# Combining two experts' outputs on one core: a new pitch of the partitions in HBM, an early activation table and last stores from SyncE

## The chip, the cores and the metric

The kernel runs on one core of a Trainium2 chip. The metric is the device time in microseconds (us) of one execution; less is better. Partitions are the 128 rows of the on-chip memory SBUF. HBM is the memory off the core, from which DMA engines bring data in and to which they take results. Each core has 16 DMA engines, and two queues feed them here: q1, filled by SyncE (SP), and q10, filled by ScalarE (ACT).

## The reference

Each of 16 x 1024 tokens has two vectors of 512 floats, the outputs of two experts, and two weights. The result is their weighted sum.

```
batch, seq, hidden, k = 16, 1024, 512, 2
weights = combine_weights[..., np.newaxis]                    # (16, 1024, 2, 1)
return np.sum(expert_outputs * weights, axis=2)               # (16, 1024, 512) float32
```

So 67.1 MB come in, 33.6 MB go out, and every loaded value is used once.

## The kernel before

The 16384 tokens are laid over the 128 partitions in blocks: partition p holds tokens 128 p to 128 p + 127. A token is 4 KB of input and 2 KB of output, so in HBM neighbouring partitions lie 512 KB apart in the input and 256 KB apart in the output; this distance is the pitch. The loop runs over 16 tiles, and each takes the next J = 8 tokens of every partition: 32 KB per partition in (`et`, 4 MB), 16 KB per partition out (`ot`, 2 MB).

The weights come as one table `wt` of 128 x 256 floats, with one DMA issued from ACT (L43). Loads of `et` are issued from SP (L48), stores from ACT (L66). `et` and `ot` have four buffers each. A load thus waits until DVE has read the buffer's last user, four tiles earlier; a tile's computation waits for its load, and for the store of four tiles before to have left the `ot` buffer. Instructions stand on each engine in the order in which the program writes them, so an engine that waits holds up all that it has to do later, its DMA issues included.

For a token, a first instruction writes the first vector times its weight to `ot`: on VectorE (DVE) as a scaling (L57), and in the last tile (g = 15) on ACT as an ACTIVATE with a scale (L55). A second one on DVE (L58) adds the other vector times its weight. ACT needs an activation table before its first ACTIVATE, and the compiler puts that load (ACT_TABLE_LOAD) right ahead of it. A tile is stored whole, but the last one in parts of 4, 2 and 2 tokens.

In what follows "store 14" is the store of tile 14, the last that is stored whole. Lines L43 to L66 are those of the kernel before; in the changed kernel L54 loads the table, L61 loads `et`, L70 is the ACTIVATE, L72 and L73 are DVE's two steps, and L82 stores.

Of the kernel before, what the change touches and what calls it, by code (L numbers as in the profile page):

```python
# [1 line left out]

# [4 lines left out]


@with_exitstack
def kernel(  # L10
    ctx: ExitStack,
    tc: tile.TileContext,
    expert_outputs: bass.AP,
    combine_weights: bass.AP,
    out: bass.AP,
):


    nc = tc.nc
    b, s, k, h = expert_outputs.shape  # L20
    assert k == 2
    n = b * s
    P = nc.NUM_PARTITIONS
    per = n // P
    assert per * P == n
    eo = expert_outputs.rearrange("b s k h -> (b s) (k h)").rearrange("(p t) f -> p t f", p=P)
    cw = combine_weights.rearrange("b s k -> (b s) k").rearrange("(p t) k -> p (t k)", p=P)
    o = out.rearrange("b s h -> (b s) h").rearrange("(p t) f -> p t f", p=P)

    dt = mybir.dt.float32  # L30
    mult = mybir.AluOpType.mult
    add = mybir.AluOpType.add

    J = 8
    copy = mybir.ActivationFunctionType.Copy
    last = per // J - 1

    wpool = ctx.enter_context(tc.tile_pool(name="w", bufs=1))
    ipool = ctx.enter_context(tc.tile_pool(name="in", bufs=4))
    opool = ctx.enter_context(tc.tile_pool(name="out", bufs=4))  # L40

    wt = wpool.tile([P, per * k], dt)
    nc.scalar.dma_start(out=wt, in_=cw)  # L43

    for g in range(per // J):
        et = ipool.tile([P, J, k * h], dt)
        ot = opool.tile([P, J, h], dt)
        nc.sync.dma_start(out=et, in_=eo[:, g * J : (g + 1) * J, :])  # L48
        c0 = 0
        for c in (4, 2, 2) if g == last else (J,):  # L50
            for i in range(c0, c0 + c):
                t = g * J + i
                w0, w1 = wt[:, 2 * t : 2 * t + 1], wt[:, 2 * t + 1 : 2 * t + 2]
                if g == last:  # L54
                    nc.scalar.activation(out=ot[:, i, :], in_=et[:, i, 0:h], func=copy, scale=w0)  # L55
                else:
                    nc.vector.tensor_scalar_mul(out=ot[:, i, :], in0=et[:, i, 0:h], scalar1=w0)  # L57
                nc.vector.scalar_tensor_tensor(  # L58
                    out=ot[:, i, :],
                    in0=et[:, i, h : 2 * h],  # L60
                    scalar=w1,  # L61
                    in1=ot[:, i, :],
                    op0=mult,
                    op1=add,
                )
            nc.scalar.dma_start(  # L66
                out=o[:, g * J + c0 : g * J + c0 + c, :], in_=ot[:, c0 : c0 + c, :]
            )
            c0 += c


# [1 line left out]
_INS = ['expert_outputs', 'combine_weights']  # L73
_OUTS = [((16, 1024, 512), 'float32')]


# [23 lines left out]
```

## Time and profile before

| what | value |
|---|---|
| median of 3 runs | 241.34 us (241.24 to 241.75) |
| the profiled execution, its own time | 241.88 us |
| its span | 240.1 us |
| DVE busy | 133.8 us (56%) |
| ACT busy | 6.4 us (3%) |
| mean over the span | 420 GB/s |
| an `et` load, issue to landing, median | 49.6 us (4096 KB) |
| a whole `ot` store, issue to landing, median | 24.9 us (2048 KB) |

The span runs from the first to the last instruction in the trace; the time of an execution holds a little more. The DMA share is the mean busy share of the 16 DMA engines. Packets are the pieces into which a DMA is cut for one engine: here one partition's row, 32 KB of a load or 16 KB of a store.

### The profile page before, as it was taken

What the parts mean: (1) busy time and instruction counts of PE and PEld (TensorE: products, weight loads), DVE (VectorE), ACT (ScalarE), POOL (GpSimd) and SP (SyncE); (2) the same over time, 40 slices, a digit from 0 to 9 for tenths busy, and PEclk for the clock granted to TensorE, in tenths of its full rate; (3) what the DMA queues carried; (4) which work ended last, traced back from release to release, by engine and by line L of the source; (5) the groups of instructions that cost most, each with busy time, mean ns of one, the idle gap of its engine ahead of it and who ended that gap; (6) DMA issues with size and microseconds to landing.
All of it is one profiled execution on the core that took longest, in us unless ns stands there. A gap on an engine that the chain in (4) does not pass through costs nothing.

```text
span 240.1 us, 377 instructions
## 1 busy us (share of the span) xinstructions
DVE 133.8 (56%) x248; ACT 6.4 (3%) x9; POOL 0.2 (0%) x4
## 2 busy tenths in 40 slices
DVE  0068937729185490945819276391853919549062
ACT  0000000000000000000000000000000000000072
POOL 0000000000000000000000000000000000000000
DMA  7999999999999999999999999999999999999967
GB/s 267 439 434 431 355 434 456 414 431 437 437 423 445 439 409 426 456 415 453 420 437 431 415 448 423 431 450 437 435 423 434 420 429 442 418 450 437 412 296 304
DMA packets 5042, 100.81 MB, mean 420 GB/s; under 512 B 560, under 2 KB 688, under 8 KB 944
## 3 DMA queue, kind: packets, MB, share of 16 engines
q1 hardware_dynamic: 2304, 67.11, 65.4%
q10 hardware_dynamic: 2736, 33.69, 32.9%
q14 instruction: 2, 0.02, 0.0%
HBM read 67.24 MB, written 33.55 MB: 420 GB/s over the span
## 4 chain that ended last, share of the span: by engine, by line
DMA 56%; DVE 26%; another core or an unknown queue 13%; issue 1%; ACT 1%; SPq 0%; ACTq 0%; DVEq 0%
DMA et<-in_expert_outputs_dram 56%; DVE ot L58 16%; DVE ot L57 10%; ACT ot L55 1%; ACT L55 1%; SPq L48 0%; ACTq L66 0%; DVEq L95 0%; DVEq L57 0%; ACTq L55 0%
## 5 line engine op out<-in xcount | busy, mean ns | idle before, releaser
L57 DVE TENSOR_SCALAR ot<-et,wt 128x512 f32<-128x512 f32 x120 | 52.7, 482 | 93.4 <-DMA et<-in_expert_outputs_dram 79.5
L58 DVE SCALAR_TENSOR_TENSOR ot<-et,wt,ot 128x512 f32<-128x512 f32 x128 | 90.0, 746 | 9.3 <-ACT ot L55 9.3
L55 ACT ACT_TABLE_LOAD x1 | 1.3, 1283 | 227.8 <-DMA et<-in_expert_outputs_dram 227.8
L55 ACT ACTIVATE ot<-et,wt 128x512 f32<-128x512 f32 x8 | 5.1, 709 | 1.5 <-DVE ot L58 1.5
L84 POOL MEMSET const-bfloat16-1.0<- 128x1 bf16 x1 | 0.1, 101 | 0.0
L84 POOL MEMSET const-uint8-127<- 128x1 uint8 x1 | 0.1, 101 | 0.0
L84 POOL MEMSET const-float32-0.0<- 128x1 f32 x1 | 0.1, 98 | 0.2 <-issue 0.2
L84 POOL MEMSET const-float32-1.0<- 128x1 f32 x1 | 0.1, 98 | 0.0
## 6 DMA issues: line engine op xcount, KB each, us to landing
et<-in_expert_outputs_dram SPq DMA_DIRECT2D x16, 4096.0 KB, 49.6
out_dram<-ot ACTq DMA_DIRECT2D x15, 2048.0 KB, 24.9
out_dram<-ot ACTq DMA_DIRECT2D x1, 1024.0 KB, 3.9
out_dram<-ot ACTq DMA_DIRECT2D x2, 512.0 KB, 3.2
wt<-in_combine_weights_dram ACTq DMA_DIRECT2D x1, 128.0 KB, 13.2
```

Source lines behind the costliest of these rows:

```text
L55: nc.scalar.activation(out=ot[:, i, :], in_=et[:, i, 0:h], func=copy, scale=w0)
L57: nc.vector.tensor_scalar_mul(out=ot[:, i, :], in0=et[:, i, 0:h], scalar1=w0)
L58: nc.vector.scalar_tensor_tensor(out=ot[:, i, :], in0=et[:, i, h : 2 * h], scalar=w1, in1=ot[:, i, :], op0=mult, op1=add,)
L84: nc = _bacc.Bacc("TRN2", target_bir_lowering=False, num_devices=1)
```

## The change

The first 15360 tokens are laid over the partitions with 120 tokens each, so that the pitch is 480 KB in and 240 KB out; they make tiles 0 to 14. The last 1024 tokens are laid out on their own with 8 tokens per partition, at a pitch of 32 KB in and 16 KB out; they make tile 15. The table is loaded in two DMAs accordingly, 960 B and 64 B per partition, both from ACT. The first token of tile 0 is scaled by an ACTIVATE on ACT, with which the activation table's load moves to the start of the kernel. The last tile is stored in four parts of two tokens, issued from SP and not from ACT.

```diff
-    eo = expert_outputs.rearrange("b s k h -> (b s) (k h)").rearrange("(p t) f -> p t f", p=P)
-    cw = combine_weights.rearrange("b s k -> (b s) k").rearrange("(p t) k -> p (t k)", p=P)
-    o = out.rearrange("b s h -> (b s) h").rearrange("(p t) f -> p t f", p=P)
+    J = 8
+    main = per - J
+    eo = expert_outputs.rearrange("b s k h -> (b s) (k h)")
+    cw = combine_weights.rearrange("b s k -> (b s) k")
+    o = out.rearrange("b s h -> (b s) h")
+
+    def rows(x):
+        a = x[0 : P * main, :].rearrange("(p t) f -> p t f", p=P)
+        b = x[P * main : n, :].rearrange("(p t) f -> p t f", p=P)
+        return lambda t, c: a[:, t : t + c, :] if t < main else b[:, t - main : t - main + c, :]
+
+    eo, cw, o = rows(eo), rows(cw), rows(o)
...
-    nc.scalar.dma_start(out=wt, in_=cw)
+    for t, c in ((0, main), (main, J)):
+        nc.scalar.dma_start(
+            out=wt[:, k * t : k * (t + c)].rearrange("p (t k) -> p t k", k=k), in_=cw(t, c)
+        )
...
-        nc.sync.dma_start(out=et, in_=eo[:, g * J : (g + 1) * J, :])
+        nc.sync.dma_start(out=et, in_=eo(g * J, J))
         c0 = 0
-        for c in (4, 2, 2) if g == last else (J,):
+        for c in (2, 2, 2, 2) if g == last else (J,):
...
-                if g == last:
+                if t == 0 or g == last:
                     nc.scalar.activation(out=ot[:, i, :], in_=et[:, i, 0:h], func=copy, scale=w0)
...
-            nc.scalar.dma_start(
-                out=o[:, g * J + c0 : g * J + c0 + c, :], in_=ot[:, c0 : c0 + c, :]
+            (nc.sync if g == last else nc.scalar).dma_start(
+                out=o(g * J + c0, c), in_=ot[:, c0 : c0 + c, :]
             )
```

More of the change, by code (lines that the diff above doesn't have):

```diff
@@ L32 @@
     add = mybir.AluOpType.add
-    J = 8
     copy = mybir.ActivationFunctionType.Copy
```

## The prediction

> **What bounds the kernel now.** I read the page first: the busy line, the DMA rows, then the queues.
>
> ```profile
> DVE 133.8 (56%) x248; ACT 6.4 (3%) x9; POOL 0.2 (0%) x4
> DMA  7999999999999999999999999999999999999967
> q1 hardware_dynamic: 2304, 67.11, 65.4%
> q10 hardware_dynamic: 2736, 33.69, 32.9%
> HBM read 67.24 MB, written 33.55 MB: 420 GB/s over the span
> ```
>
> No compute engine is busy for more than 56%. The 16 DMA engines are: q1 (loads) and q10 (stores and the weight table) hold 65.4 + 32.9 = 98.3% of 16 x 240.1 us, so 236.0 us of the 240.1 us on a mean DMA engine. Only 4.1 us per engine are not transfer. The kernel is bound by DMA from end to end, and what the change can win lies in those 4.1 us or in packets that last longer than they must.
>
> For the second I go to the trace's single DMA records. Of the 2048 load packets of 32 KB at least three in four last exactly 1213 ns, the shortest; all stores of 16 KB lie between 611 and 626 ns. 32 KB in 1213 ns is 27.0 GB/s, times 16 it is 432 GB/s. So at the present 512 KB pitch nearly every packet already takes one fixed minimum. Sorted by engine (each engine's packets abut, so they can be strung together), the excess over 1213 ns is alike on all: about 0.69 us in the very first load packet, about 0.74 us in the load packets around the first store (23 to 28 us), then nearly nothing, 1.57 us on a mean engine in all. The second patch is the one dip of the GB/s row, in the second line below; the windows also show the hole at the end:
>
> ```profile
> 0.00:6.00 6.00, 0.00 (x0) 0.00 (x0) 0.20 (x4) 1.00 0.74 268
> 24.00:30.00 6.00, 6.00 (x12) 0.00 (x0) 0.00 (x0) 1.00 0.93 355
> 210.00:216.00 6.00, 2.82 (x6) 0.00 (x0) 0.00 (x0) 1.00 1.04 448
> 228.00:231.00 3.00, 1.15 (x2) 2.99 (x5) 0.00 (x0) 1.00 0.98 421
> 231.00:234.00 3.00, 2.92 (x5) 1.88 (x4) 0.00 (x0) 1.00 0.42 175
> 234.00:237.00 3.00, 1.42 (x2) 1.33 (x2) 0.00 (x0) 1.00 0.99 404
> ```
>
> The last two columns are the DMA share and GB/s. From 231 to 234 us the share is 0.42: 0.58 x 3 = 1.7 us of hole per mean engine. The timeline says why:
>
> ```profile
> 221.78 0.34 ACTq L66 DMA_DIRECT2D out_dram<-ot  x1
> 227.81 1.28 ACT L55 ACT_TABLE_LOAD   x1 [227.81 <-DMA et<-in_expert_outputs_dram]
> 229.10 3.78 ACT L55 ACTIVATE ot<-et,wt 128x512 f32<-128x512 f32 x6
> 229.85 4.07 DVE L58 SCALAR_TENSOR_TENSOR ot<-et,wt,ot 128x512 f32<-128x512 f32 x6 [8.11 <-ACT ot L55]
> 232.63 1.66 ACTq L66 DMA_DIRECT2D out_dram<-ot  x2
> 234.34 1.33 ACT L55 ACTIVATE ot<-et,wt 128x512 f32<-128x512 f32 x2 [1.46 <-DVE ot L58]
> 235.09 1.42 DVE L58 SCALAR_TENSOR_TENSOR ot<-et,wt,ot 128x512 f32<-128x512 f32 x2 [1.17 <-ACT ot L55]
> 236.54 0.34 ACTq L66 DMA_DIRECT2D out_dram<-ot  x1
> ```
>
> The last load lands, the table is loaded (1.28 us), four tokens are computed, and the first store of the last tile goes out only at 232.63. Then ACT waits for DVE to issue the second store before it goes on.
>
> The mean hides one thing. In the records 15 engines finish store 14 between 231.4 and 232.6 us and wait in the hole, but one finishes at 233.35, and the next store's packets reach it at 233.46. It is the one on which both 8 KB instruction fetches (q14) fall, at 47.4 and 173.6 us: each leaves a gap of 0.3 us there and stretches the next load packet by 0.5 to 0.6 us. **This engine never sees the hole.** Every store and load needs all 16 engines, so it sets the end.
>
> **The change, part by part**, against the profiled execution: span 240.1, time 241.88, so 1.78 us lie around the span. The median of the shown runs is 241.34, 0.54 below; I apply the sum to it.
>
> *Table load early* (L70, token 0 on ACT). It moves 1.28 us from 227.8 to about 14 us, when tile 0 has landed; behind it on ACT are one ACTIVATE (0.7 us, ready near 16) and store 0, not due before 22. DVE takes token 0's product fifth, near 13.9 + 3 x 0.44 + 2 x 0.66 = 16.5, so it does not wait. Cost 0; without that cover store 0 would be late, and the load queue still has loads 1 to 3 then. DVE does one scaling less in tile 0, 0.44 us, hidden because DMA bounds.
>
> *Last stores in four parts of two tokens, from SyncE* (L82). SP has nothing after its last load at 177.4 but the end, so its four waits hold up no one; ACT keeps 8 ACTIVATEs without a wait between. They start at 227.81, the first is done at 228.54, DVE follows at 4.07 / 6 = 0.68 each and ends at 228.56 + 8 x 0.68 = 234.0 instead of 236.5. The first pair is stored at about 229.95, reaches the engines 0.83 us later (232.63 to 233.46 before), at 230.8, well before store 14 is done on any of them. The hole closes. The chain by compute is then: last issue 234.05, + 0.9 to its packets, + 1.3 for them = 236.3; before it was 238.8. That would be 2.5 us.
>
> But what is late next is the slow engine's own work: store 14 till 233.35, then 32 packets of 4 KB. Before, it had 8 of 8 KB and 16 of 4 KB after that, and gaps of only 0.10 and 0.27 us, waiting for the two issues. The gaps go, -0.37 us; 16 packets of 0.162 us in place of 8 of 0.318 are +0.04; four completion records instead of three +0.01. So **-0.32 us** on the engine that counts, not 1.7 or 2.5.
>
> *Second table transfer* (L54): 8 more packets per engine of 64 B, one more completion record. The trace has 46 ns for 1 KB and 9 ns for 4 B; 64 B lies nearest to the latter, so I take 11 ns, 0.09 us with the record; the bound is 8 x 46 = 0.37. It shares its queue's turn with load 1, as the first shares load 0's (landing at 13.9), and lands near 23 us; nobody reads it before 227. Tile 0 waits for the first transfer alone.
> The Trainium skill, "DMA: Bandwidth & Descriptors", Specifications, speaks against this edit: below 512 B a DMA does a read-modify-write. The 1 KB and 4 B records above show no threshold; a price for 64 B no run here shows.
>
> *Pitch 512 to 480 KB in, 256 to 240 KB out; the last tile 32 and 16 KB.* Bytes, packets and their sizes stay. Since packets last 1213 and 611 ns at the old pitch, and these are the fixed minimum of the trace, I price it at 0. Bounds: below, both patches of excess vanish, -0.69 - 0.74 = -1.43 us; above, the excess of a first packet falls on each of an engine's 8 packets of the last tile, 8 x 0.69 = +5.5 us.
> The skill, same page, "Latency and other measured facts", gives 207 GB/s for a 512 KiB pitch against 214 for a padded one. By that, 236.0 x 7 / 214, an estimate, is 7.7 us of gain, a time near 234. This case's 432 GB/s within packets leaves no such loss; the rows decide.
>
> Sum: -0.32 + 0.09 + 0 = -0.2 us; 241.34 - 0.2 = **241.1 us**.
>
> **Rivals.**
> *A. The pitch removes the slow patches.* For it: in both, all engines lose about the same within a few microseconds, as when partition rows collide. Against it: each engine loses it once, at its first read and at its first store, and its 120 or so other load packets at the same pitch lose nothing; that looks like an empty pipeline. One patch gone: 241.1 - 0.7 = 240.4; both: 239.7.
> *B, slower: SP's queue has never stored.* q10's first store cost every engine 0.74 us, and its packets came 4 to 6 us after the issue at 22.5, not 0.9. If q1's first store costs the same, it falls in the tail, on the slow engine, where nothing covers it: 241.1 + 0.74 = 241.9. It decides once it exceeds the 0.2 us saved. Against it: the time was lost in load packets, and there are no loads in the tail.
> *C, slower: the last tile at 32 KB pitch reads worse*: 241.1 + 5.5 = 246.6 at the worst. Nothing in the trace has this pitch; the tile's 128 packets are as long as the others.
> *D. The slow engine is not slow in the changed run*, if the instruction fetches fall on different engines: then the second slowest, 232.6 instead of 233.35 at the end of store 14, sets the end: 240.4.
>
> **How the numbers follow.** My forecast 0.56 (its own range 240.7 to 241.6: +0.28 if the 64 B packets cost the most, -0.4 and +0.3 for the spread of the runs, which is 0.5), A 0.20, D 0.07, B 0.13, C 0.04. About 0.2% (0.48 us) is what a measurement can tell here: faster is below 240.86, slower above 241.82. Faster: A, D and a sixth of the forecast, 0.36. Slower: B, C and a little of the forecast, 0.20. Same: 0.44. The range takes in all of A down to 239.7, and B with the forecast's upper spread, 242.1; C and chance lie outside.
>
> **What would show it.** Right: table load near 14 us, last-tile ACTIVATEs at one stretch, last issue near 234 on SP, DMA share near 0.8 or more in the three microseconds that had 0.42, span about 239.9, and one DMA engine still the last. A shows as a GB/s row without the dip near 24 to 30 us and a first slice above 268. B shows as a share below 0.8 after 230 us although stores are issued; C as the last load landing some microseconds late. I am wrong if the span falls below 238.4, or rises, with the tail's issues in place.

## The result and the profile after

The changed kernel took 241.26 us (median of 6 runs, 241.20 to 241.44), the kernel before 241.55 in the same comparison: ratio 0.9989, 95% interval 0.9976 to 1.0002 (all ratios here are of the means, and against the kernel before in the same comparison). A second comparison, with twelve runs of the changed kernel, gave 241.33 against 241.21: ratio 0.9999, interval 0.9991 to 1.0008. So the change makes no difference that can be told, and 241.1 us was predicted. Its profiled execution took 241.23 us, with a span of 239.5.

The page after, the same rows:

```profile
DVE 133.3 (56%) x247; ACT 7.0 (3%) x10; POOL 0.2 (0%) x4
DMA  7999899999999999999999999999999999999995
GB/s 268 451 441 439 350 438 476 401 432 424 411 441 435 479 394 438 435 441 400 435 438 441 435 460 413 438 402 432 437 435 479 397 438 427 449 397 435 438 409 213
q1 hardware_dynamic: 2880, 69.21, 67.6%
q10 hardware_dynamic: 2448, 31.59, 30.9%
q14 instruction: 2, 0.02, 0.0%
```

2 MB of stores have gone from q10 to q1; the sum is 98.5%, and the kernel is still bound by DMA. The first slice is at 268 GB/s and the fifth (24 to 30 us) at 350, so both slow patches are where they were. The windows (the last two columns are DMA share and GB/s) and the timeline of the tail:

```profile
24.00:30.00 6.00, 6.00 (x13) 0.00 (x0) 0.00 (x0) 1.00 0.91 358
228.00:231.00 3.00, 2.67 (x5) 3.00 (x6) 0.00 (x0) 1.00 1.01 431
231.00:234.00 3.00, 2.72 (x5) 1.58 (x3) 0.00 (x0) 1.00 0.90 370
234.00:237.00 3.00, 0.00 (x0) 0.00 (x0) 0.00 (x0) 1.00 0.84 341
```

```profile
13.37 1.28 ACT L70 ACT_TABLE_LOAD   x1 [13.37 <-DMA et<-in_expert_outputs_dram]
221.64 0.34 ACTq L82 DMA_DIRECT2D out_dram<-ot  x1
227.58 5.01 ACT L70 ACTIVATE ot<-et,wt 128x512 f32<-128x512 f32 x8 [212.19 <-DMA et<-in_expert_outputs_dram]
228.33 5.39 DVE L73 SCALAR_TENSOR_TENSOR ot<-et,wt,ot 128x512 f32<-128x512 f32 x8 [6.72 <-ACT ot L70]
229.77 4.31 SPq L82 DMA_DIRECT2D out_dram<-ot  x4
```

The tail runs as planned: the table is loaded at 13.4 us, the eight ACTIVATEs run without a break, the last store is issued near 233.8 us in place of 236.5, and the hole is closed (DMA share 0.90 in place of 0.42). And the time stays. The DMA records, sorted by engine, say why: 15 engines are done between 236.3 and 236.6 us, as the compute chain would allow. The one that carries both instruction fetches (47.2 and 173.5 us, almost the same moments as before) finishes store 14 at 233.11 us, against 231.3 to 231.6 on the others, and ends at 238.1, with no gap in between.

### The profile page after: what moved, and what is told of

The parts are those of the page before. It is cut to its first block, busy times and chain, and to the rows that moved or that the text cites. A ratio compares the mean times of both kernels' runs of the same rounds, so it can differ in the third digit from the quotient of the medians.

```text
span 239.5 us, 382 instructions
## 1 busy us (share of the span) xinstructions
DVE 133.3 (56%) x247; ACT 7.0 (3%) x10; POOL 0.2 (0%) x4
## 4 chain that ended last, share of the span: by engine, by line
DMA 56%; DVE 26%; another core or an unknown queue 13%; issue 1%; SPq 0%; ACT 0%; DVEq 0%; ACTq 0%
DMA et<-in_expert_outputs_dram 56%; DVE ot L73 17%; DVE ot L72 10%; SPq L61 0%; ACT ot L70 0%; DVEq L111 0%; ACTq L82 0%; DVEq L72 0%; ACTq L70 0%
## 5 line engine op out<-in xcount | busy, mean ns | idle before, releaser
L70 ACT ACTIVATE ot<-et,wt 128x512 f32<-128x512 f32 x9 | 5.7, 709 | 212.2 <-DMA et<-in_expert_outputs_dram 212.2
L70 ACT ACT_TABLE_LOAD x1 | 1.3, 1283 | 13.4 <-DMA et<-in_expert_outputs_dram 13.4
```

## The experiments

**The parts of the change alone.** The first has the new layout and both table DMAs with the old tail; the second has the new tail at the old pitch.

```diff
 # e1_pitch, against the changed kernel
-        for c in (2, 2, 2, 2) if g == last else (J,):
+        for c in (4, 2, 2) if g == last else (J,):
-                if t == 0 or g == last:
+                if g == last:
-            (nc.sync if g == last else nc.scalar).dma_start(
+            nc.scalar.dma_start(
```

> Only the new layout (480 KB pitch, contiguous last tile, two table DMAs); the tail is the old one: parts of 4, 2, 2 from ACT, activation table loaded late. My theory (the pitch is free, because the packets last 1213 and 611 ns at either pitch): same as the kernel before to within 0.3 us, +0.1 us for the 64 B packets; first-packet excess of about 0.7 us per engine at the start and 0.5 to 0.7 us at the first store still there. Rival A (the pitch removes slow patches): 0.7 to 1.4 us faster than before. Rival C (the contiguous last tile reads worse): the last load lands late, up to 5 us slower.

```diff
 # e2_tail, against the kernel before: the reverse of the three edits above
```

> Only the tail and the early table, at the old 512 KB pitch. My theory: this is all of the gain, 0.3 us (0.2 to 0.5) faster than before, and as fast as the changed kernel. If the tail were bound by the compute chain (table load, ACT and DVE), it would be 2.5 us faster; if the pitch carried the gain, it would equal the kernel before.

e1_pitch: 241.74 us against 241.32, ratio 1.0009 (1.0000 to 1.0018). e2_tail: 241.31, ratio 0.9997 (0.9987 to 1.0007). The layout gains nothing, so rival A falls: 97% of the load packets in the changed kernel last 1213 to 1216 ns at 480 KB, as at 512 KB, and both patches stay (0.69 and 0.74 us per engine before; 0.73 and 0.53 after). The 64 B packets took 11 ns each. Of e2_tail I had expected 0.3 us, and it is not there in the medians either.

The single times say more than the medians. Those of the kernel before in this comparison lie in two groups: 12 of 21 between 241.04 and 241.34, and 9 between 241.70 and 241.90. e1_pitch, with the same old tail, has 9 of 11 in the upper group (above 241.6); whether the new layout makes this group more frequent, or chance did, these runs do not settle. e2_tail has 10 of 11 below 241.6, and the changed kernel all of its 18. **The tail edits do not shift the lower group; they take away nearly all of the upper one.** My first trace of before, with 241.88 us, was one of the upper group. From its packets against those of e1_pitch's trace (241.29 us) I formed a theory: the order in which the slow engine takes loads and stores differs by one packet, and in one of the two orders the old chain by compute is late.

**Half of the tail each.**

```diff
 # e5_table, against the kernel before
-                if g == last:
+                if t == 0 or g == last:
 # e6_sp, against the kernel before
-        for c in (4, 2, 2) if g == last else (J,):
+        for c in (2, 2, 2, 2) if g == last else (J,):
-            nc.scalar.dma_start(
+            (nc.sync if g == last else nc.scalar).dma_start(
```

> The kernel before with the early activation table alone (token 0 of tile 0 on ACT). My theory: the old tail's times fall into two groups, 241.2 and 241.8 us, because the last load lands on the slow DMA engine either with 12 or with 11 store packets of 16 KB still ahead of the last tile's; in the second case the chain by compute is 0.4 to 0.5 us too late for that engine. The chain 1.3 us shorter is early enough in both cases: all runs near 241.25 us, the upper group gone. Rival (the two groups come from elsewhere, the tail has no part in them): groups as before, median 241.3 to 241.5.

> The kernel before with the last stores alone: four parts of two tokens from SP, the activation table still loaded late. My theory: the first part is issued at about 231.3 and the last at 235.3 us, 1.2 us sooner than before; again early enough for the slow engine in both cases: all runs near 241.25 us, upper group gone. Rival (only the table load counts): groups as before. If SP's first store cost 0.7 us (rival B), all runs near 241.9 us.

e5_table: 241.31 us, eleven runs from 241.14 to 241.41. e6_sp: 241.34, eleven from 241.20 to 241.49. The kernel before beside them: 27 runs, of which 8 above 241.6. In these eleven runs each, either half alone removes the upper group, both together do no more, and the lower group does not get faster. SP's first store costs nothing: in the changed kernel its packets last 159 ns and on the slow engine they abut, so rival B falls.

**The kernel before once more, for its other group.**

> The kernel before once more, for a second trace of it. My theory of the two groups: if its time is near 241.2 us, the slow DMA engine has 12 or more packets of 16 KB to store after its last load packet and no gap of 0.1 us or more between store 14 and the parts of the last tile; if near 241.8 us, it has 11 and gaps of 0.3 to 0.4 us in all, as in the first trace. Rival: the groups differ elsewhere (more slow packets, a third fetch), and the order of the packets at the end is the same in both.

This execution took 241.13 us, one of the lower group. Windows and timeline of the tail:

```profile
231.00:234.00 3.00, 2.12 (x4) 1.55 (x3) 0.00 (x0) 1.00 0.64 270
```

```profile
220.98 0.34 ACTq L66 DMA_DIRECT2D out_dram<-ot  x1
231.83 1.66 ACTq L66 DMA_DIRECT2D out_dram<-ot  x2
235.74 0.34 ACTq L66 DMA_DIRECT2D out_dram<-ot  x1
```

All is 0.8 us earlier than in the first trace. The slow engine still ends store 14 at 233.13 us (233.35 in the first trace), but it has 12 packets of 16 KB to go after its last load packet instead of 11. The last load so lands one store packet, 0.61 us, sooner relative to the engine's remaining work. The stores of the last tile are therefore there in time, and the gaps of 0.10 and 0.27 us are 0. The hole on the other engines is there in both groups, and costs nothing by itself in either. This is as the theory says; it rests on one trace of before for each group, with e1_pitch's as a third (12 packets, no gap of 0.1 us).

Two further readings of the traces belong here. In the upper-group trace all 16 engines end between 238.69 and 238.84 us, so there the late last store set the end, and the slow engine waited for it too; in the lower-group trace the slow engine is last, at 238.10, shortly after the others (237.88 to 238.05). And the gaps are not the whole distance of the groups: of the 0.64 us by which the slow engine ends sooner, 0.37 are the gaps and 0.22 lay already at the end of store 14. e2_tail's trace (241.43 us) has the new tail, 11 packets and no gap, but ends store 14 at 233.33 us like the first trace. So the new tail is in time in this order too; where the 0.22 us come from stays open.

**Every tile contiguous.** The table DMA stays in the old layout here, so a token's weights are not its own; the traffic is that of the kernel but for the table.

```diff
 # e7_contig, against the changed kernel
+        v = x.rearrange("(g p t) f -> g p t f", p=P, t=J)
+        return lambda t, c: v[t // J, :, t % J : t % J + c, :]
```

> The changed kernel with every tile laid out as its last one: contiguous 4 MB in, 2 MB out, pitch 32 and 16 KB, one table DMA. My theory (packets at their minimum whatever the pitch): same as the changed kernel to within 0.2 us, 241.1 to 241.4. Rival C (32 KB pitch reads worse): packets above 1213 ns and some us slower. Rival A (a pitch that is a large power of two costs the slow patches): 0.7 to 1.4 us faster than the kernel before.

241.27 us, ratio 0.9996 (0.9987 to 1.0005). Rival C falls, and with 32, 480 and 512 KB alike the pitch is free here. In the trace of this kernel, and in that of the changed one, the load packets of the last tile last 1213 ns (1216 at most).

**Is it the engine with the fetches that sets the end?** One kernel with more DVE instructions, and three with fewer.

```diff
 # e4_morefetch, against the changed kernel, tiles 0 to 14, each token
+                    for _ in range(2):
+                        nc.vector.memset(tiny, 0.0)
```

> The changed kernel with two tiny DVE memsets (one float per partition) per token more in tiles 0 to 14: 240 more instructions, DVE still far from busy, so that about two more instruction fetches come in the span. My theory: two more fetches on the same engine, 0.85 us each, 1.7 us slower than the changed kernel, about 243.0 us. Rival (fetches do not set the end): no change, 241.2 us; if the extra fetches fall on other engines, less than 0.3 us.

```profile
span 241.3 us, 622 instructions
DVE 147.1 (61%) x487; ACT 7.0 (3%) x10; POOL 0.2 (0%) x4
q14 instruction: 4, 0.03, 0.0%
```

243.29 us, 2.0 more than the changed kernel. There are four fetches in place of two, DVE is still idle for 39% of the span, and the slowest engine ends store 14 at 234.91 us in place of 233.11, while most others end it near 231.5 as before: 0.9 us per added fetch on that engine, 1.0 in the medians (0.9 between the two profiled executions).

```diff
 # e3_nofetch, against the changed kernel (shortened): tiles 0 to 14, whole tile (tile 0 keeps token 0 on ACT)
+            nc.vector.tensor_tensor(out=ot, in0=et[:, :, 0:h], in1=w[:, :, 0:1].to_broadcast(...), op=mult)
+            nc.vector.tensor_tensor(out=et[:, :, h:], in0=et[:, :, h:], in1=w[:, :, 1:2].to_broadcast(...), op=mult)
+            nc.vector.tensor_tensor(out=ot, in0=et[:, :, h:], in1=ot, op=add)
```

> The changed kernel with three DVE instructions per tile (weights broadcast along the row, whole tile at once) in tiles 0 to 14, in place of 15 or 16: some 55 DVE instructions in place of 247, so that no instruction fetch falls on a DMA engine inside the span. My theory (the one engine that carries both fetches sets the end): q14 has no packet in the span, all engines end alike, and the time falls by the lag of the slow engine, 1.5 us (1.2 to 1.9), to 239.7 us. Rival (the slow engine's lag is covered by others' work, the end is set by the last tile's chain): no change from the changed kernel, 241.2 us.

```profile
q14 instruction: 1, 0.01, 0.0%
226.10 0.34 ACTq L77 DMA_DIRECT2D out_dram<-ot  x1
```

240.55 us, ratio 0.9962 (0.9950 to 0.9975), half of the gain that I expected. The lag is nearly gone: 15 engines end store 14 between 231.9 and 232.0 us, and the last at 232.4, after a fetch at 226.6. But DVE needs 13.1 us for a tile in place of 8.6, and store 14 is issued at 226.1, not 221.6; 15 engines then stand still for 0.1 to 0.6 us near 227. That this took the other half of the gain is argued here; e8_best avoids the standstill.

```diff
 # e8_best, against the changed kernel (shortened): tiles 0 to 13 (tile 14 as tile 15: scaled on ACT;
 # one ACTIVATE on a column of the weights keeps the table load early)
+            e2 = et.rearrange("p j (k h) -> p (j k) h", k=k)
+            nc.vector.tensor_tensor(out=e2, in0=e2, in1=w.to_broadcast([P, J * k, h]), op=mult)
+            nc.vector.tensor_tensor(out=ot, in0=et[:, :, 0:h], in1=et[:, :, h : 2 * h], op=add)
 # e9_fewer: tile 14 in these two instructions as well
```

> The changed kernel with two DVE instructions per tile in tiles 0 to 13 (both vectors times their weights in place, broadcast along the row, then one addition), and tile 14 computed as tile 15, scaled by ACT: 44 DVE instructions in all. In e3_nofetch the lag of the slow engine was gone, but store 14 was issued 4.5 us later than before and left a hole of 0.2 to 0.5 us on all engines, and one fetch still came at 226.6 us. My theory: no fetch in the span, no hole, all engines end alike: 239.9 us (239.6 to 240.3). Rival (e3's gain of 0.7 us is all there is; the end is set by something else): 240.5 us.

> e8_best with tile 14 also in two DVE instructions (38 in all). In e8_best the span fell to 238.1 us, but the time outside the span grew from 1.7 to 2.1 us, with an instruction fetch at 239.2 us, after the span. My theory: that late fetch is what the time outside the span grew by; with 6 instructions fewer it does not come, the span stays near 238.1 us and the time is 239.85 us (239.7 to 240.1). Rival (the 0.4 us has another cause): 240.3 us.

In e8_best no fetch is left in the span, and all engines end between 236.4 and 236.8 us (237.0 to 237.3 in e3_nofetch). The span is 238.1, 1.4 less than the changed kernel's. The time is 240.31 us, ratio 0.9961 (0.9949 to 0.9974), since 2.1 us and not 1.7 to 1.8 lie around the span (in all five runs), with a fetch at 239.2 us in the trace. e9_fewer gives 240.09 us, ratio 0.9953 (0.9939 to 0.9967), with a span of 238.3 and 1.8 us around it, and no fetch from the span's start on. Two of its six runs lie higher, at 240.6 and 240.7, with a longer span; why, no trace shows. The median lies 1.1 us below that of the kernel before and 1.2 below that of the changed one.

```profile
span 238.3 us, 174 instructions
DVE 201.3 (84%) x38; ACT 6.7 (3%) x10; POOL 0.2 (0%) x4
GB/s 269 453 443 435 440 327 432 435 440 479 429 413 399 437 440 440 432 426 462 396 437 481 402 407 473 440 396 437 459 391 429 484 435 402 440 418 418 437 407 300
```

DVE is 84% busy with 38 instructions, where it was 56% busy with 247: the slower computation gives the faster kernel. The dip has moved from the fifth slice to the sixth (327 GB/s), with tile 0's store, which is issued some 5 us later here than in the changed kernel.

**What the dip is.**

```diff
 # e10_warm, against e9_fewer
+    nc.vector.memset(warm, 0.0)
+    nc.scalar.dma_start(out=o(0, 1)[:, 0, 0:128], in_=warm)
```

> e9_fewer with one small extra store (128 x 512 B of zeros to places that tile 0's store overwrites later) from ACT's queue ahead of the second table load, so that the queue's first store comes near 13 us and not near 25. It asks what the slow patch at the first store is. If it is the cost of the queue's first write, 0.5 to 0.8 us per engine of load excess show near 13 us and none at tile 0's store; if it belongs to the first long store beside the loads, it stays where it was. The time is e9_fewer's to within 0.3 us in both cases.

The small store's packets ran from 13.6 to 22.9 us, and load packets that start between 3 and 22 us lost 0.01 us per engine. At tile 0's store they lost 0.62 us per engine. So it is not the queue's first write, but belongs to the first long store beside the loads; what it is stays open. The time missed my bound: 241.10 us, 1.0 more than e9_fewer. The trace's timeline shows where most of it went:

```profile
191.88 4.67 ACTq L73 DMA_DIRECT2D out_dram<-ot  x2
207.23 8.69 DVE L71 TENSOR_TENSOR et<-et,wt 128x8192 f32<-128x8192 f32 x1 [2.44 <-DMA et<-in_expert_outputs_dram]
215.84 8.75 DVE L72 TENSOR_TENSOR ot<-et 128x4096 f32<-128x4096 f32 x2
```

DVE does two tiles' products and then their two additions, so that no store is issued from 196.2 to 221.9 us; the store queue runs dry and every engine stands for 0.7 to 1.3 us near 222.8. In e9_fewer the same order leaves next to no gap (its next store is issued at 220.8): it lies just at that edge. Another 0.1 us lies around the span: 1.9 us in all ten runs, though this trace has no fetch from the span's start on.

**The changed kernel again.**

> The changed kernel once more, unaltered, for the groups: all runs between 241.1 and 241.5 us, against two groups (near 241.2 and 241.8) of the kernel before; its median 0 to 0.2 us below that of before. Rival (the tail gains on all runs): its runs lie 0.3 us below the lower group of before, at 240.9.

Twelve runs from 241.18 to 241.49, one group; median 241.33. Beside it 20 of 23 runs of the kernel before were below 241.5 (most near 241.2), and 3 above 241.6. The group is as expected, the sign of the small difference is not: with so few upper runs the kernel before is no slower. Against the lower group alone the changed kernel is about 0.1 us slower, which is as much as the 64 B packets and the smaller parts were priced at; that these are its cause is not shown.

## Why the prediction was right, and where not

- *The bound.* Right for the changed kernel: one DMA engine, the one with both fetches, sets the end; e4_morefetch and the kernels with fewer instructions move the time as this requires. The step "the slow engine's own work is late next" is what kept the forecast from 2.5 us. In the profiled execution before, this engine was not last: it too waited for the last stores and ended with the rest.
- *Pitch at 0.* Right, by e1_pitch and e7_contig. The row of the Trainium skill that the prediction weighed ("DMA: Bandwidth & Descriptors", "Latency and other measured facts", on row pitch) is for copies between HBM tensors; by it the prediction's estimate was 7.7 us of gain. For the loads and stores here no such gain shows (e1_pitch 1.0009, e7_contig 0.9996); the packets of 1213 ns decided rightly.
- *64 B packets at 11 ns.* Right to the nanosecond, in 128 of 128 packets; nothing dearer shows for them.
- *Table load early at no cost; SP's first store at no cost.* Right.
- *The tail, -0.32 us.* **The term that was mis-sized.** The gaps of 0.10 and 0.27 us on the slow engine were read from one execution and applied to the median. They exist in the upper group only. There the tail edits gain about 0.5 us (from near 241.8 to 241.3); in the lower group the gaps are 0 and the gain is nothing. The base of the sum, 241.34 us, was a run of the lower group, and there the gain does not apply: all 18 runs of the changed kernel lie above the 241.1 us forecast, the lowest at 241.18. On the mean over the groups, with 3 to 9 upper runs in some 20 to 27, that is 0.1 to 0.2 us, so the sum came out near by the mix of the groups, which is luck and not insight. The median shows it only when the groups are nearly even, as in the first comparison. Against the profiled execution before, the span fell by 0.6 us and not by the 0.2 of the sum: the slow engine ended store 14 0.24 us sooner, which the sum did not have, and the gaps went.
- *The spread of before* (241.24 to 241.75 in three runs) was in the prediction as noise of 0.5 us. It was two groups; the traces hold a cause for the larger part of their distance, the gaps of 0.37 us.
- *Rival D* (fetches on another engine): both fell on one engine in the traces, at the same moments, as before.

## What to carry to other kernels

When a kernel is bound by DMA, look at each DMA engine and not at their mean: a hole that 15 of 16 engines see costs nothing if the sixteenth never has it, and closing it gains nothing. A stream of some hundred small instructions on a compute engine can cost transfer time by its own fetches (0.9 us each here), so fewer and longer instructions may pay even where they keep that engine busy for longer. And before a gap of some tenths of a microsecond is put into a sum, see whether the runs of the kernel fall into groups, and take a trace of each.

## What the runs showed of the hardware that was not expected

An instruction fetch of 8 KB took 0.31 us on its DMA engine, but stretched the next load packet by 0.53 to 0.65 us too, and cost 0.9 to 1.0 us of time in e4_morefetch. With a fetch at 239.2 us, after the span, the time around the span was 2.1 us (e8_best), and without it 1.8 (e9_fewer). That the fetch is the cause is not shown: e10_warm, without one, has 1.9. In the two kernels, e9_fewer and e10_warm the load packets lost, in sum, 0.5 to 0.75 us per engine once, when the first whole-tile store started, near 26 us in the two kernels and some 5 us or more later in the other two; a small store before it did not take this away.
